# Two transformer blocks on one core: norm steps divided between two engines with order ties, attention and state-space projections in another order, the first loads on another queue, and the last rows in two groups

## The chip, the cores and the metric

One core of a Trainium2 chip. The metric is the time of one execution in microseconds of device time; the kernel before has a median of 2513.2 us over 3 runs (2512.42 to 2513.47).

The core's engines run side by side, each through its own list of instructions in order: TensorE (PE in the rows; its weight loads PEld), VectorE (DVE), ScalarE (ACT), GpSimd (POOL) and SyncE (SP). An engine goes on past an instruction only when what it waits for from the others has come. Loads are issued from a queue, SP's (SPq) or ScalarE's (ACTq).

## What is computed

Two blocks one after the other on one sequence of 256 tokens of width 2048. The parts that the change touches:

```python
# first block
h = rmsnorm(x, g_mix);  z = h @ w_in          # cb, cc, cv, q, k, v, f, gate_c, gate_a
...
x = x + (relu(rmsnorm(x, g_mlp) @ w_ff1) ** 2) @ w_ff2
x = rmsnorm(x, g_final)
# second block
h = rms_norm(x, norm_mix_g) * (1 + scale_m) + shift_m        # h3 in the kernel
q, k, v, xs, z, bmat, cmat, dt = split(h @ w_in_2)
attn = rms_norm(moba_attention(q, k, v, rel_bias), attn_norm_g)
ssm = ssd_mixer(xs, z, bmat, cmat, dt, ...)                  # gated by silu(z), then a norm
x = x + gate_m * (concat([attn, ssm]) @ w_out)
h = rms_norm(x, norm_ffn_g) * (1 + scale_f) + shift_f        # h4 in the kernel
x = x + gate_f * ((silu(g) * val) @ w_down)                  # g, val = conv(h @ w_up)
return rms_norm(x, final_norm_g)
```

`c`'s modulation (shift, scale, gate) comes from `w_ada`. Everything is float32.

## The kernel before

**Products.** Each weight is streamed once, in pieces of 128 x 2048 floats. `piece` (L102) loads one on SP's queue; ScalarE rounds it into `wH` (L122) and VectorE forms the rest `wL` (L123); three buffers of each. An activation is kept as a pair too: `h` and `l`, side by side. `mm` (L129) issues every matmul: a `wH` block against the pair at once (512 columns) and a `wL` block against `h` alone (256 columns, or 512 where the pair lies the other way). `bblock`, `wide` (L186) and `ablock` go over the pieces of a product. In `wide` with `lo_first` all matmuls that need only `h` and `wL` of the first half of the pieces run first.

**The order.** A scheduler lays out each engine's list beforehand, by its own estimate of durations and by a priority of issue. `behind` (L131) adds a tie: an instruction has to come later in the list of its engine than another. `piece` takes such a tie as `hold` for its first quarter's `wL`.

**Start.** `wide` of `cc0` at L443 asks `h1_tiles` (L432) for two 128-row tiles of `x` ahead of each quarter of the first weight piece: a load on SP's queue, then ScalarE's `h` (L436) and VectorE's `l` (L437), both scaled by `g_mix`, the first 16 columns of `vec`. The squares of `x` for the norm (L448 to L456) run at high priority.

**Norms.** `norm2` (L329) makes h3 and h4 from four 512-column chunks of x. Per chunk i: two copies `xc` (L336, VectorE; one for each half t of the tokens) scaled by 1/rms, transposes on TensorE into `trh` (L344), then for each 128-row tile `h` on ScalarE (L350), `nt` on VectorE (L352) and `l = nt - h` on VectorE (L354). 1/rms takes a power on GpSimd (L277, L709). `held` keeps the `l` of tile 7 as a tie for the piece of the second group of k tiles. `conv4` (L714, tiles `bcsp`) is the first user of h3, `up(0)` (L923) of h4.

**Second attention and state space.** Loop L859 goes over j = 0, 1: q and k (each a `bblock`), during each of which `ssm_decay` (tiles `d`, `m`) runs and after it `ssm_out` (tiles `yp`); then v (`ablock`), then `heads` (L421; logits `s`, softmax, transposed `pt`, output `o`, copied to `cat` at L872). `rms_ch` (L829) squares `cat` on ScalarE, adds up on VectorE (L836), sums over channels on TensorE (`rattp`), takes the power on GpSimd, and spreads the result over the partitions (`rattbp`, L282; read back on ScalarE, L284). Then come z0 and z1 (`bblock`, silu at L881, product with `cat` at L883), `cat_split` (L840; scaling at L848, `h` L304, `l` L305; result `catA`), and `wo`, the product with `w_out`, that reads `catA`. `gm_bc` and `gf2` spread modulation over the partitions: 32 transposes (L293) in 8 banks, read by ScalarE (L294).

**End.** `down_last` (L955) does the last four products for both token halves t: `tm` (L970), x (L971), square (L325), product with the final gain (L974), 1/rms, scaling (L980 to L986), and a store of 512 columns each (L987).

Of the kernel before, what the change touches and what calls it, by code (L numbers as in the profile page):

```python
# [25 lines left out]
for _n, _w in (("g_mix", 16), ("b_gate", 32), ("conv_w", 24), ("g_mlp", 16), ("b_ada", 96),  # L26
# [9 lines left out]
def body(ctx: ExitStack, tc: tile.TileContext, x_d, xT_d, vec_d, con_d, rel_d, relc_d, gfin_d, c_d, fg_d,  # L36
# [149 lines left out]
    def wide(W, halves, acts, name, dst, post=None, feed=None, lo_first=False,  # L186
# [13 lines left out]
        for kg in range(2):  # L200
# [128 lines left out]
    def norm2(src, r, av, bv, name):  # L329
        acts = []  # L330
        for i in range(4):
            h, l, hl = act_chunk(name, i)
            xs = []
            for t in range(2):
                xc = tp.tile([P, 512], F32, tag="t2k", bufs=4, name="xc")
                V.tensor_scalar(xc, src[i][:, t, :], r[:, t:t + 1], None,  # L336
                                op0=OP.mult)
                xs.append(xc)
            for b in range(2):
# [6 lines left out]
                for k in range(2):  # L346
# [82 lines left out]
    h1 = []  # L429
    sq0 = []  # L430

    def h1_tiles(h, l, hl, k0, k1):  # L432
        load(xT[:, k0:k1, :], xT_d[:, k0:k1, :])
        for kt in range(k0, k1):
            k = kt % 4
            A.activation(h[:, k, :], xT[:, kt, :], AF.Copy, scale=vc("g_mix", kt))  # L436
            V.scalar_tensor_tensor(l[:, k, :], xT[:, kt, :], vc("g_mix", kt),  # L437
# [8 lines left out]
    load(vec[:, 16:], vec_d[:, 16:])  # L446
    load(con, con_d)
    with tc.high_priority():  # L448
        sacc = junk().rearrange("p (a s) -> p a s", a=2)
        for i in range(8):  # L450
            if i == 0:
                A.activation(sacc, xT[:, 0:2, :], AF.Square)
            else:
                sq = tp.tile([P, 2, S], F32, tag="t2k", bufs=4, name="sq0")
                A.activation(sq, xT[:, 2 * i:2 * i + 2, :], AF.Square)
# [258 lines left out]
    def conv4(nb, ch0, name, first=False):  # L714
        raw = q4([P, 4, S], name + "r")
        if first:
            wide(win2_d, (2 * nb, 2 * nb + 1), h3, name + "p", lambda i: (raw, i), lo_first=True,
                 hold=held["h3"])
# [139 lines left out]

    for j in range(2):  # L859
        qk = []  # L860
# [6 lines left out]
        qT, kT = qk  # L867
# [4 lines left out]
        heads(j, qT, kT, vt, toep, lambda h, o: V.tensor_copy(cat[:, h, :], o))  # L872
# [48 lines left out]
    ss4 = cp.tile([P, 2, 4], F32, name="ss4")  # L921

    def up(j):  # L923
        raw = q4([P, 4, S], f"up{j}r")
        if j == 0:
            wide(wup_d, (0, 1), h4, "up0", lambda i: (raw, i), lo_first=True, hold=held["h4"])
# [28 lines left out]
    def down_last(c, u):  # L955
        ws = [piece(wdn_d[n, c], 4, extra=None if n < 3 else True) for n in range(4)]
        rs4 = cp.tile([P, 2], F32, name="rs4")
        for t in range(2):
            ts = slice(t * P, (t + 1) * P)
            for n in range(4):  # L960
                h, l = ws[n]
                cs = slice(n * 512, (n + 1) * 512)
# [142 lines left out]
```

## Time and profile before

| | us |
|---|---|
| median of 3 runs | 2513.2 |
| the profiled execution | 2515.24 |
| its span (first to last instruction) | 2513.5 |
| TensorE busy | 2481.0 (99%) |
| VectorE busy | 1824.1 (73%) |
| ScalarE busy | 1188.8 (47%) |
| GpSimd busy | 8.0 (0%) |

The columns of a timeline row: start, length, engine, line, operation, out<-in, shapes and how many instructions the row takes together; in brackets the idle time of the engine ahead of it and what ended that. The length of a matmul reaches past the start of the next one: what counts is the distance from start to start. All times are from the span's start.

### The profile page before, as it was taken

Reading aid. Unit: us, or ns where it says so; the run is one execution under the profiler, and the core shown is the slowest. Engines: PE = TensorE matmul, PEld = TensorE weight load, DVE = VectorE, ACT = ScalarE, POOL = GpSimd, SP = SyncE. Lnnn points to the kernel's source line nnn. Section 1 sums busy time; section 2 is a strip of 40 time slices with the busy share of each in tenths; the row PEclk is TensorE's granted clock in tenths of the full one; section 3 lists DMA queues with packets and bytes.
Section 4 is the critical chain, followed back from the end, with each engine's and each line's share of the span. In section 5 each row is a group of like instructions: output and inputs, shape, how many; then the busy total and the mean of one; then the engine's idle time right before and its main releaser. Section 6 shows DMA issues by size and latency. Waiting matters only on the chain.

```text
span 2513.5 us, 31941 instructions
## 1 busy us (share of the span) xinstructions
PE 2481.0 (99%) x13202; PEld 2137.0 (85%) x13202; DVE 1824.1 (73%) x2011; ACT 1188.8 (47%) x1265; POOL 8.0 (0%) x16
## 2 busy tenths in 40 slices
PE   8999999999999999999998999999999999999998
PEld 7888888888888888888887888888888888888887
DVE  6787777787777777777756776575777777777768
ACT  6444444544544444444445544464544444444444
POOL 0000000000000000000000000000000000000000
PEclk9999999999999999999999999999999999999999
DMA  7677776678777777777656444455455555555553
GB/s 283 251 272 282 269 265 254 239 281 315 277 282 278 282 286 271 283 285 280 255 191 210 168 168 161 158 187 198 151 196 192 199 199 187 185 187 195 187 201 118
DMA packets 84977, 573.55 MB, mean 228 GB/s; under 512 B 9368, under 2 KB 10464, under 8 KB 16864
## 3 DMA queue, kind: packets, MB, share of 16 engines
q1 hardware_dynamic: 80352, 564.16, 61.4%
q10 hardware_dynamic: 4480, 7.36, 0.9%
q8 instruction: 103, 1.69, 0.3%
q14 instruction: 42, 0.34, 0.0%
HBM read 567.27 MB, written 4.21 MB: 227 GB/s over the span
## 4 chain that ended last, share of the span: by engine, by line
PE 96%; DVE 2%; ACT 1%; DMA 1%; issue 0%; POOL 0%; SPq 0%; ACTq 0%; POOLq 0%
PE ff L129 27%; PE up L129 20%; PE dn L129 9%; PE ga L129 4%; PE gc L129 4%; PE q L129 4%; PE k L129 4%; PE v L129 3%; PE wo L129 3%; PE mix L129 3%; PE cc L129 3%; PE z L129 2%; PE cb L129 2%; PE co L129 1%; PE ao L129 1%; PE xsc0p L129 1%
## 5 line engine op out<-in xcount | busy, mean ns | idle before, releaser
L123 DVE TENSOR_TENSOR wL<-wraw,wH 128x2048 fp32r<-128x2048 f32 (+1 forms) x511 | 998.5, 1963 | 532.8 <-ACT wH L122 524.1
L122 ACT ACTIVATE wH<-wraw 128x2048 fp32r<-128x2048 f32 (+1 forms) x511 | 837.8, 1653 | 1075.0 <-PE ff L129 359.6
L129 PE MATMUL up<-h4A,wH 128*128 128x512 f32 x1408 | 344.0, 391 | 0.0
L129 PEld LDWEIGHTS up<-h4A,wH 128*128 128x128 f32 x1408 | 256.6, 188 | 48.6 <-DVE up0r L179 0.2
L129 PE MATMUL ff<-g_mlpA,wH 128*128 128x512 f32 x1024 | 250.4, 392 | 0.0
L99 DVE SCALAR_TENSOR_TENSOR wada<-wada,c_bc 128x2048 f32<-128x2048 f32 x96 | 219.6, 2287 | 27.6 <-DMA wada<-in_wada 26.7
L129 PEld LDWEIGHTS ff<-g_mlpA,wH 128*128 128x128 f32 x1024 | 186.6, 188 | 35.7 <-issue 0.6
L129 PEld LDWEIGHTS up<-h4A,wL 128*128 128x128 f32 x1408 | 187.4, 192 | 10.3 <-ACT h4A L350 0.2
L129 PE MATMUL ff<-wH,uh 128*128 128x512 f32 x496 | 193.1, 390 | 0.0
L129 PE MATMUL ff<-wH,ul 128*128 128x512 f32 x496 | 192.9, 389 | 0.0
L129 PE MATMUL up<-h4A,wL 128*128 128x256 f32 x1408 | 191.3, 284 | 0.0
L129 PE MATMUL dn<-wH,vhl 128*128 128x512 f32 x640 | 158.3, 389 | 0.0
L129 PEld LDWEIGHTS ff<-g_mlpA,wL 128*128 128x128 f32 x1024 | 135.4, 191 | 7.4
L129 PEld LDWEIGHTS dn<-wH,vhl 128*128 128x128 f32 x640 | 119.5, 188 | 24.4
L129 PE MATMUL ff<-g_mlpA,wL 128*128 128x256 f32 x1024 | 137.9, 283 | 0.0
L129 PE MATMUL ff<-wL,uh 128*128 128x512 f32 x496 | 127.7, 389 | 0.0
L129 PEld LDWEIGHTS ff<-wH,uh 128*128 128x128 f32 x496 | 93.2, 188 | 19.4 <-issue 0.2
L129 PEld LDWEIGHTS ff<-wH,ul 128*128 128x128 f32 x496 | 93.1, 188 | 19.4 <-issue 0.2
L129 PEld LDWEIGHTS ff<-wL,uh 128*128 128x128 f32 x496 | 93.1, 188 | 19.4
L129 PE MATMUL dn<-wL,vhl 128*128 128x512 f32 x320 | 85.5, 389 | 0.0
L129 PEld LDWEIGHTS dn<-wL,vhl 128*128 128x128 f32 x320 | 60.1, 188 | 12.5
L129 PE MATMUL ga<-h1A,wH 128*128 128x512 f32 x256 | 64.6, 396 | 1.3 <-DVE aos L179 1.3
(559 smaller groups left out, 3172.2 us busy)
## 6 DMA issues: line engine op xcount, KB each, us to landing
wraw<-in_wff SPq DMA_DIRECT2D x128, 1024.0 KB, 4.8
wraw<-in_win SPq DMA_DIRECT2D x106, 1024.0 KB, 4.8
wada<-in_wada SPq DMA_DIRECT2D x96, 1024.0 KB, 4.8
wraw<-in_wup SPq DMA_DIRECT2D x88, 1024.0 KB, 4.8
wraw<-in_wdn SPq DMA_DIRECT2D x44, 1024.0 KB, 4.8
wraw<-in_wv SPq DMA_DIRECT2D x16, 1024.0 KB, 4.8
wraw<-in_wmix SPq DMA_DIRECT2D x16, 1024.0 KB, 4.9
wraw<-in_wout SPq DMA_DIRECT2D x16, 1024.0 KB, 4.8
```

Of the source, the lines that this page charges most:

```text
L99: V.scalar_tensor_tensor(w, w, 1.0, c_bc, op0=OP.mult, op1=OP.mult, accum_out=mod[:, i:i + 1])
L122: A.activation(h[:, sl], raw[:, sl], AF.Copy)
L123: ins = V.tensor_tensor(l[:, sl], raw[:, sl], h[:, sl].bitcast(F32), op=OP.subtract)
L129: return T.matmul(o, l, r, start=first, stop=last, skip_group_check=True)
```

## The change

- **Start.** `g_mix` moves from `vec` into 16 columns in front of `x` (`xTg`), so the small first load is gone. The loads of `x` for k0 = 0 and 2 are issued by ScalarE. The squares of `x` are tied behind the last `h` of `x`.
- **Norms.** In `norm2`, `xc` of the first token half is made by ScalarE for chunks 1 to 3, and `nt` of odd tiles as well. `hold` becomes a pair: the first `wL` of the second half's first piece comes behind `xc` of chunk 0, second token half; the first `wL` of the second group stays behind `l` of tile 7.
- **Second attention.** q0, k0, q1, k1 with their state-space parts come first, then v0, heads 0, v1, heads 1.
- **End.** The last 512 columns of the second token half are computed as two groups of 256; squares are summed in five columns (`ss4`, zeroed at its making), the final gain is multiplied in ahead of the scaling everywhere, and two stores of 1024 columns replace four of 512 for each token half.

```diff
     def wide(...):
             if kg == 0 and lo_first:
-                ws = [piece(W[hf, kg], 4, nt=8) for hf in halves]
+                ws = [piece(W[hf, kg], 4, nt=8, hold=hold[0] if hold and i else None)
+                      for i, hf in enumerate(halves)]
...
-                             hold=hold if kg == 1 and i == 0 else None)
+                             hold=hold[1] if hold and kg == 1 and i == 0 else None)
...
     def norm2(...):
-                V.tensor_scalar(xc, src[i][:, t, :], r[:, t:t + 1], None,
-                                op0=OP.mult)
+                if t == 0 and i > 0:
+                    A.activation(xc, src[i][:, t, :], AF.Copy, scale=r[:, t:t + 1])
+                else:
+                    held[name] = V.tensor_scalar(xc, src[i][:, t, :], r[:, t:t + 1], None,
+                                                 op0=OP.mult)
+                    if i == 0:
+                        held[name + "0"] = held[name]
...
-                    V.tensor_scalar(tt, ps[:, k * S:(k + 1) * S], av[:, kt:kt + 1],
-                                    bv[:, kt:kt + 1], op0=OP.mult, op1=OP.add)
+                    if k:
+                        A.activation(tt, ps[:, k * S:(k + 1) * S], AF.Identity,
+                                     bias=bv[:, kt:kt + 1], scale=av[:, kt:kt + 1])
+                    else:
+                        V.tensor_scalar(tt, ps[:, k * S:(k + 1) * S], av[:, kt:kt + 1],
+                                        bv[:, kt:kt + 1], op0=OP.mult, op1=OP.add)
...
     def h1_tiles(h, l, hl, k0, k1):
-        load(xT[:, k0:k1, :], xT_d[:, k0:k1, :])
+        c0, c1 = (16 if k0 else 0) + k0 * S, 16 + k1 * S
+        if k0 < 4:
+            A.dma_start(xTg[:, c0:c1], xT_d[:, c0:c1])
+        else:
+            load(xTg[:, c0:c1], xT_d[:, c0:c1])
...
-                A.activation(sacc, xT[:, 0:2, :], AF.Square)
+                behind(A.activation(sacc, xT[:, 0:2, :], AF.Square), h1_last[0])
...
+    qk = []
     for j in range(2):
-        qk = []
         for hq, (nb, nm, sc) in enumerate(((0 + j, f"q2{j}", SCALE), (2 + j, f"k2{j}", None))):
...
-        qT, kT = qk
+    for j in range(2):
         ps = ablock(wv2_d, j, range(4), h3, f"v2{j}")
...
-        heads(j, qT, kT, vt, toep, lambda h, o: V.tensor_copy(cat[:, h, :], o))
+        heads(j, qk[2 * j], qk[2 * j + 1], vt, toep, lambda h, o: V.tensor_copy(cat[:, h, :], o))
...
     def down_last(c, u):
+                cuts = ((0, 512),) if t == 0 or n < 3 else ((0, 256), (256, 512))
+                for j, (a, b) in enumerate(cuts):
...
+                    V.tensor_tensor(tm[:, a:b], ps[:, a:b], gf2[:, cs], op=OP.mult)
+                    V.tensor_tensor(x3[:, t, cs], x3[:, t, cs], tm[:, a:b], op=OP.add)
+                    A.activation(junk()[:, a:b], x3[:, t, cs], AF.Square, accum_out=ss4[:, t, n + j:n + j + 1])
+                    if t and n == 3:
+                        y3 = tp.tile([P, 512], F32, tag="t2k", bufs=4, name="y3") if j == 0 else y3
+                        V.tensor_tensor(y3[:, a:b], x3[:, t, cs], fg[:, cs], op=OP.mult)
+                    else:
+                        V.tensor_tensor(x3[:, t, cs], x3[:, t, cs], fg[:, cs], op=OP.mult)
...
-                nc.sync.dma_start(out[0, ts, cs], x3[:, t, cs])
+                if n % 2:
+                    cs = slice((n - 1) * 512, (n + 1) * 512)
+                    nc.sync.dma_start(out[0, ts, cs], x3[:, t, cs])
```

What the scheduler makes of it is seen in the engines' lists, which hold instructions in the order in which they run. First ScalarE from its first instruction, before (`wH_96` and `h1A_85` are the first weight piece and the first four tiles of `x`):

```order
L71 DMA vec<-in_vec 128x16
L88 ACT_TABLE_LOAD
L88 ACTIVATE warm<-mhalf 128x2
L452 ACTIVATE junk<-xT 128x512
L436 ACTIVATE h1A_85<-xT,vec 128x256 x2
L122 ACTIVATE wH_96<-wraw_95 128x512
```

and now (L453 is `h`, L448 the load of `x`):

```order
L448 DMA xT<-in_xT 128x528
L88 ACT_TABLE_LOAD
L88 ACTIVATE warm<-mhalf 128x2
L448 DMA xT<-in_xT 128x512
L122 ACTIVATE wH_95<-wraw_94 128x512
L453 ACTIVATE h1A_84<-xT 128x256 x2
```

The square has left the start, the second load of `x` stands behind the table load, and the first `wH` quarter is now ahead of the first `h`.

VectorE at the step from the first block's end to h3, before (L705 to L708 are sums for the two norms, L651 a square, `wL_10535` the piece of `conv4`'s second half):

```order
L123 TENSOR_TENSOR wL_10535<-wraw_10533,wH_10534 128x512 x2
L705 TENSOR_REDUCE ra<-ssa 128x1
L651 SCALAR_TENSOR_TENSOR sqx,ssb<-xg_10292 128x512
L336 TENSOR_SCALAR xc<-x_4636,rb 128x512
L706 TENSOR_SCALAR re<-ra 128x1
L707 TENSOR_REDUCE rb<-ssb 128x1
L275 TENSOR_SCALAR ra<-ra 128x2
L708 SCALAR_TENSOR_TENSOR rb<-rb,re 128x1
L336 TENSOR_SCALAR xc<-x_4636,rb 128x512 x5
L352 TENSOR_SCALAR nt<-trh_10321,am,mod 128x256
```

and now (L340 is `xc`, L362 `nt`, L722 to L725 the sums):

```order
L668 SCALAR_TENSOR_TENSOR sqx,ssb<-xg_10291 128x512
L340 TENSOR_SCALAR xc<-x_4635,rb 128x512
L722 TENSOR_REDUCE ra<-ssa 128x1
L724 TENSOR_REDUCE rb<-ssb 128x1
L723 TENSOR_SCALAR re<-ra 128x1
L725 SCALAR_TENSOR_TENSOR rb<-rb,re 128x1
L276 TENSOR_SCALAR ra<-ra 128x2
L340 TENSOR_SCALAR xc<-x_4635,rb 128x512 x2
L123 TENSOR_TENSOR wL_10458<-wraw_10456,wH_10457 128x512
L123 TENSOR_TENSOR wL_10534<-wraw_10532,wH_10533 128x512 x3
L340 TENSOR_SCALAR xc<-x_4635,rb 128x512
L362 TENSOR_SCALAR nt<-trh_10320,am,mod 128x256
```

Three quarters of `wL` that stood ahead of the sums, with one more, now stand between the `xc` of the second token half and the first `nt`.

TensorE from the last `o` of `heads` (`pT` against `vt`) to the sum of squares `rattp` of the attention's norm, before:

```order
L129 MATMUL z_0_12717<-h3A_10378,wH_12757 128x512 x4
L129 MATMUL o_12442<-pT,vt_12347 128x256
L129 MATMUL o_12442<-pT,vt_12347 128x128
L129 MATMUL z_0_12717<-h3A_10409,wH_12757 128x512 x4
L129 MATMUL z_0_12717<-h3A_10378,wL_12758 128x256 x4
L129 MATMUL z_0_12717<-h3A_10409,wL_12758 128x256 x4
L129 MATMUL z_1_12798<-h3A_10316,wH_12800 128x512 x8
L129 MATMUL z_1_12798<-h3A_10347,wH_12800 128x512 x8
L129 MATMUL z_1_12798<-h3A_10316,wL_12801 128x256
L129 MATMUL rattp<-con,ratta 128x1 x2
```

and now (`z_1` is the last half block of z, and the last row the first four of the 32 transposes for `gm_bc` and `gf2`):

```order
L129 MATMUL z_1_12797<-h3A_10408,wL_12838 128x256 x4
L129 MATMUL z_1_12797<-h3A_10377,wH_12837 128x512 x4
L129 MATMUL o_12441<-pT,vt_12346 128x256
L129 MATMUL o_12441<-pT,vt_12346 128x128
L129 MATMUL z_1_12797<-h3A_10408,wH_12837 128x512 x4
L129 MATMUL z_1_12797<-h3A_10377,wL_12838 128x256 x4
L129 MATMUL z_1_12797<-h3A_10408,wL_12838 128x256 x4
L129 MATMUL rattp<-con,ratta 128x1 x2
L283 MATMUL rattbp<-con,rattr 128x128 x2
L294 MATMUL gm_bcp_12480<-con,mod 128x128 x4
```

Before, 29 matmuls of z stood between the last `o` and `rattp`, then 36 more up to `rattbp`, and 11 more ahead of the first `wo`, with 28 of the 32 transposes around them. Now 12 stand ahead of `rattp`, none of z comes after it, and `rattbp` follows at once. Between `rattbp` and the first `wo` there are now the 32 transposes and `rss0p` (two matmuls); between the first and the second matmul of `wo` there is `rss0bp`, the spread of the first state-space norm.

## Rows read from the trace of the kernel before

**Rows 1.** The page's chain that ended last: shares of the span by engine.

```profile
PE 96%; DVE 2%; ACT 1%; DMA 1%; issue 0%; POOL 0%; SPq 0%; ACTq 0%; POOLq 0%
```

**Rows 2.** TensorE's waits: line, waited for, total us, times, longest us.

```profile
PE trh L344 <- DVE xc L336: 5.4, 3, 3.1
PE trh L344 <- DVE re L706: 4.3, 1, 4.3
PE yp L129 <- DVE m L806: 2.0, 1, 2.0
```

**Rows 3.** Stretches: length, busy PE, PEld, DVE, ACT, POOL, granted clock, DMA, GB/s.

```profile
1377.00:1384.00 7.00, 4.46 (x20) 4.06 (x21) 5.71 (x19) 2.23 (x5) 1.21 (x2) 0.51 0.22 84
1384.00:1390.00 6.00, 5.93 (x46) 5.35 (x45) 6.00 (x16) 3.66 (x8) 0.00 (x0) 1.00 0.01 3
1766.00:1773.00 7.00, 5.05 (x24) 5.06 (x25) 6.28 (x17) 3.06 (x6) 0.55 (x1) 0.51 0.00 0
```

**Rows 4.** Timeline of the start: TensorE and ScalarE.

```profile
6.20 2.08 PE L129 MATMUL cc<-h1A,wH 128*128 128x512 f32 x4 [6.20 <-ACT wH L122]
...
8.59 4.44 PE L129 MATMUL cc<-h1A,wH 128*128 128x512 f32 x12 [0.31 <-DVE h1A L437]
...
10.96 0.63 ACT L122 ACTIVATE wH<-wraw 128x512 fp32r<-128x512 f32 x1
```

**Rows 5.** Timeline of the step to h3: VectorE, GpSimd, TensorE.

```profile
1376.17 1.28 DVE L123 TENSOR_TENSOR wL<-wraw,wH 128x512 fp32r<-128x512 f32 x2
...
1380.12 2.18 DVE L336 TENSOR_SCALAR xc<-x,rb 128x512 f32<-128x512 f32 x5 [1.27 <-POOL rb L709]
1382.22 0.54 DVE L352 TENSOR_SCALAR nt<-trh,am,mod 128x256 f32<-128x256 f32 x1
...
1383.13 1.99 PE L129 MATMUL bcsp<-h3A,wL 128*128 128x256 f32 x12
...
1378.87 0.70 POOL L277 TENSOR_TENSOR ra<-ra,mhalf 128x2 f32<-128x2 f32 x1 [3.91 <-DVE rb L708]
```

**Rows 6.** Timeline of the step to h4: VectorE.

```profile
1764.60 1.89 DVE L123 TENSOR_TENSOR wL<-wraw,wH 128x512 fp32r<-128x512 f32 x3
...
1767.41 2.18 DVE L336 TENSOR_SCALAR xc<-x,rs 128x512 f32<-128x512 f32 x5 [0.66 <-POOL rs L277]
...
1769.50 0.54 DVE L352 TENSOR_SCALAR nt<-trh,af,mod 128x256 f32<-128x256 f32 x1
```

**Rows 7.** Timeline from the last `o` to `wo`: TensorE, ScalarE, VectorE.

```profile
1656.33 0.81 PE L129 MATMUL o<-pT,vt 128*128 128x256 f32 x4
...
1658.85 3.82 PE L129 MATMUL z<-h3A,wH 128*128 128x512 f32 x16
1662.50 0.28 PE L129 MATMUL z<-h3A,wL 128*128 128x256 f32 x1
1662.62 0.50 PE L129 MATMUL rattp<-con,ratta 128*128 128x1 f32 x4
...
1669.03 1.47 PE L293 MATMUL gm_bcp<-con,mod 128*128 128x128 f32 x12
...
1659.54 1.90 ACT L122 ACTIVATE wH<-wraw 128x2048 fp32r<-128x2048 f32 x1
...
1669.67 1.58 ACT L294 ACTIVATE gm_bc<-gm_bcp 128x512 f32<-128x512 f32 x3
...
1653.86 1.23 DVE L883 TENSOR_TENSOR cat<-cat,zs 128x1024 f32<-128x1024 f32 x1 [1.44 <-ACT zs L881]
...
1661.48 2.29 DVE L123 TENSOR_TENSOR wL<-wraw,wH 128x2048 fp32r<-128x2048 f32 x1 [0.94 <-ACT wH L122]
...
1669.65 3.26 DVE L848 SCALAR_TENSOR_TENSOR cat<-cat,vec,rattb 128x256 f32<-128x256 f32 x8 [2.24 <-ACT rattb L284]
1672.82 0.68 DVE L305 TENSOR_TENSOR catA<-cat,catA 128x512 fp32r<-128x512 f32 x1
```

**Rows 8.** Timeline of the last columns: VectorE.

```profile
2505.74 0.68 DVE L974 TENSOR_TENSOR x<-x,fg 128x512 f32<-128x512 f32 x1
```

More of the change, by code (lines that the diff above doesn't have):

```diff
@@ L25 @@
 _o = 0
-for _n, _w in (("g_mix", 16), ("b_gate", 32), ("conv_w", 24), ("g_mlp", 16), ("b_ada", 96),
+for _n, _w in (("b_gate", 32), ("conv_w", 24), ("g_mlp", 16), ("b_ada", 96),
                ("norm_mix_g", 16), ("attn_norm_g", 8), ("conv_ssm_w", 48), ("conv_ssm_b", 12),
@@ L445, in body @@
          feed=lambda q: h1_tiles(*chunks[q // 2], 2 * q, 2 * q + 2))
-    load(vec[:, 16:], vec_d[:, 16:])
+    load(vec, vec_d)
     load(con, con_d)
@@ L717, in conv4 @@
             wide(win2_d, (2 * nb, 2 * nb + 1), h3, name + "p", lambda i: (raw, i), lo_first=True,
-                 hold=held["h3"])
+                 hold=(held["h30"], held["h37"]))
         else:
@@ L957, in down_last @@
         rs4 = cp.tile([P, 2], F32, name="rs4")
+        ss4 = cp.tile([P, 2, 5], F32, name="ss4")
+        V.memset(ss4, 0.0)
         for t in range(2):
@@ L961, in down_last @@
                 h, l = ws[n]
-                cs = slice(n * 512, (n + 1) * 512)
                 ps = bank(f"dnl{t}{n}")
-                for k in range(4):
-                    mm(ps, u[k][0][:, ts], h[:, k, :], k == 0, False)
-                    mm(ps, u[k][1][:, ts], h[:, k, :], False, False)
-                for k in range(4):
-                    mm(ps, u[k][0][:, ts], l[:, k, :], False, k == 3)
-                tm = tp.tile([P, 512], F32, tag="t2k", bufs=4, name="tm")
-                V.tensor_tensor(tm, ps, gf2[:, cs], op=OP.mult)
-                V.tensor_tensor(x3[:, t, cs], x3[:, t, cs], tm, op=OP.add)
-                ss_chunk(x3[:, t, cs], ss4, t, n)
-                if n < 3:
-                    V.tensor_tensor(x3[:, t, cs], x3[:, t, cs], fg[:, cs], op=OP.mult)
+                cuts = ((0, 512),) if t == 0 or n < 3 else ((0, 256), (256, 512))
+                for j, (a, b) in enumerate(cuts):
+                    for k in range(4):
+                        mm(ps[:, a:b], u[k][0][:, ts], h[:, k, a:b], k == 0 and j == 0, False)
+                        mm(ps[:, a:b], u[k][1][:, ts], h[:, k, a:b], False, False)
+                    for k in range(4):
+                        mm(ps[:, a:b], u[k][0][:, ts], l[:, k, a:b], False, k == 3)
+                    cs = slice(n * 512 + a, n * 512 + b)
+                    tm = tp.tile([P, 512], F32, tag="t2k", bufs=4, name="tm")
+                    V.tensor_tensor(tm[:, a:b], ps[:, a:b], gf2[:, cs], op=OP.mult)
[6 more added lines that the diff above has]
+                        V.tensor_tensor(x3[:, t, cs], x3[:, t, cs], fg[:, cs], op=OP.mult)
             r = rs4[:, t:t + 1]
@@ L979, in down_last @@
                 cs = slice(n * 512, (n + 1) * 512)
-                if n == 3:
-                    V.scalar_tensor_tensor(x3[:, t, cs], x3[:, t, cs], r, fg[:, cs],
-                                           op0=OP.mult, op1=OP.mult)
-                elif n == 1:
-                    V.tensor_scalar(x3[:, t, cs], x3[:, t, cs], r, None, op0=OP.mult)
-                else:
-                    A.activation(x3[:, t, cs], x3[:, t, cs], AF.Copy, scale=r)
-                nc.sync.dma_start(out[0, ts, cs], x3[:, t, cs])
+                src = y3 if t and n == 3 else x3[:, t, cs]
+                if n in (1, 3):
+                    V.tensor_scalar(x3[:, t, cs], src, r, None, op0=OP.mult)
+                else:
+                    A.activation(x3[:, t, cs], src, AF.Copy, scale=r)
+                if n % 2:
+                    cs = slice((n - 1) * 512, (n + 1) * 512)
+                    nc.sync.dma_start(out[0, ts, cs], x3[:, t, cs])
     us = {0: up(0), 1: up(1), 2: up(2)}
```

23 lines of the change are left out of this document (13 added, 10 removed).

## The prediction

> **What bounds the kernel now.** I read the page's chain first: 96% of the span's end hangs on TensorE [rows 1]. So an edit is worth what it takes from TensorE's waits or adds to them, and nothing else that it does to VectorE or ScalarE counts. Next come TensorE's waits by their releaser [rows 2]. Three of them lie where the change works: at the norm steps TensorE waits 5.4 us for `xc` (three times) and 4.3 us for `re`, one of the sums ahead of `xc`; in the second attention it waits 2.0 us for the state-space product `m` (once). Together that is 11.7 us of 2513.5: even a change that took all of it away would be worth 0.5%. Third, the stretches around the two norm steps: the granted clock there is 0.51, the lower of TensorE's two levels (1.2 instead of 2.4 GHz), after TensorE had stood idle [rows 3]. A wait therefore costs more than its length: the first matmuls behind it run slowly. Last I read the timelines around each edit [rows 4 to 8], and beside them the lists of the engines, to see what stands between what is ready and what waits for it.
>
> Times are those of one profiled execution of 2515.24 us, with a span of 2513.5 us. It is 2.0 us above the median of 2513.2 us. I sum against 2515.24 and carry the difference to the median. About 0.2% (5 us: 2508.2 to 2518.2) is what a measurement of this kernel can tell from no change.
>
> **Start: -0.4 us.** Before, the first matmul ran at 6.20 us and the twelve others of the first piece from 8.59 us, behind the second weight quarter; the last quarter's `wH` began at 10.96 us, right after that quarter had landed [rows 4]. Now the two first weight quarters are issued ahead of x on SP, so the second quarter should be there over a microsecond earlier. The other side: ScalarE's first `wH` (0.63 us, as the last one [rows 4]) and VectorE's first `wL` stand ahead of the first `h` and `l`, so the first matmul comes some 0.7 us later, at about 6.9 us. The second x load waits behind ScalarE's table load, but its tiles are needed only from the third quarter on. The end of the piece hangs on the last quarter, and the bytes ahead of it are the same but for the small vector load. I take -0.4, between +0.7 (the first matmul's delay goes through) and -1.0 (part of TensorE's wait between its first four matmuls and 8.59). The squares that leave ScalarE's start took their place while weights were awaited, so they count nothing. The Trainium skill, page "DMA: Bandwidth & Descriptors", section "Issuing engines are not separate DMA queues", says that transfers started by several engines run on the same 16 DMA engines and interleave, and that this saves only the time of issuing. By it the term would be about 0 and the sum 0.4 us higher.
>
> **Step to h3: -0.9 us.** Three quarters of `wL` leave the way to the sums: two take 1.28 us, so three take 1.9 [rows 5]. On GpSimd, the power of `ra` (0.70 us) ran ahead of the one that the norm needs [rows 5]; in the new list it is behind. Part of the two overlaps; `xc` of the second half, at 1380.12 before, comes some 2.3 us earlier, at 1377.8. But now four quarters of `wL` (4 x 0.64 = 2.6 us) stand behind two `xc` (0.43 each, five took 2.18) and ahead of the next `xc` and the first `nt`: 1377.8 + 0.9 + 2.6 + 0.2 = 1381.5, where 1382.22 stood [rows 5]. The tie moved the work from ahead of the norm into its middle. That is 0.7; with half of the `nt` on ScalarE a further 0.2 on the way to the last `l`. Between ends: -2.3 if `wL` there delays nobody, +0.8 if ScalarE, which now makes `xc`, `h` and half of the `nt`, becomes the one that is waited for.
>
> **Step to h4: 0.** Three `wL` (1.89 us) stood ahead of the sums; `xc` followed at 1767.41 and `nt` at 1769.50 [rows 6]. `xc` comes about 0.9 us earlier, since the square on ScalarE bounds it next; then four `wL` (2.6 us) come again ahead of `nt`, which lands at about 1770. ScalarE's share of the later `nt` gives that back. Between -0.9 (all of the gain in `xc`) and +0.8 (all of the delay of `nt`).
>
> **State space in the second attention: -2.0 us.** TensorE waited 2.0 us for `m` [rows 2], where a list of short products had no weight matmuls between `d` and `yp`. Now 64 weight matmuls stand there (half at 0.228, half at 0.12: some 11 us) and no heads run beside. The wait goes whole; nothing bounds TensorE next there.
>
> **Last heads to `wo`: +6.0 us, a new wait.** The heads of j = 1 used to run beside z0, and all of z1 covered what follows them: sum of squares, power, spread, eight scalings, splits. Now heads 0 run beside v1 and z0, heads 1 beside z0 and z1, and only 12 matmuls of z are left behind the last `o`. I put the new list on the clock of before, with the last `o` at 1656.33 [rows 7].
>
> - TensorE: its 12 matmuls end at 1658.85, where z1 began before. What is left to do ahead of the second matmul of `wo` is `rattp` 0.4, `rattbp` 0.2, 32 transposes at 0.10 (twelve in about 1.25) 3.3, `rss0p` 0.4, a `wo` and `rss0bp` 0.4: 4.7 us. If nothing waited, that matmul would run at 1663.5.
> - ScalarE: `rattp`'s sum passes VectorE and GpSimd (0.70, as in [rows 5]) and `rattbp` is done at about 1660.5, but a `wH` stands ahead of the readback, 1659.54 to 1661.44, and a copy from z. The readback ends at 1662.4.
> - VectorE: a `wL` of 2.29 us from 1661.48 stands ahead as well, then 0.69 for z: free at 1664.4. Then the eight scalings 3.26, `cat` times z 1.23, the first split 0.68 [rows 7]: 1669.5.
> - ScalarE beside it: eight readbacks of the transposes and a silu at 0.53 each (three took 1.58) and `h`: 1668. VectorE is last.
>
> 1669.5 - 1663.5 = 6.0. It can't go: with nothing ahead on any engine, power, readback, scalings, product and split take 0.7 + 0.5 + 3.3 + 1.2 + 0.7 = 6.4 us from 1659.3, which is 1665.7 and 2.2 too late. So 2.2 is the lower end; 6.5, if ScalarE's row slips by one operation, is the upper. I take 6.0, since `wH` and `wL` stand in the list ahead.
>
> **The clock behind it: +1.0 us.** The clock fell at both norm steps, where TensorE had stood still or done a few transposes [rows 3]; here it stands or does short transposes for some 10 us. The price of the slow stretch: at the start, twelve matmuls took 0.37 us each from start to start (4.44 with 0.39 for the last) where z runs at 0.228 (16 in 3.65 [rows 7]): 1.7 us in all. At h3 the products ran from 1383.13 [rows 5] and the stretch from 1384 on is at full clock [rows 3], so the loss was under 0.9 x 0.5 = 0.4. I take the middle, 1.0, between 0 and 1.7. The Trainium skill, "TensorE: Matmul & The Clock Gate", section "Loop structure matters more than you think", says that a copy out of PSUM between tiles doesn't let the matmuls go cold. By that the 32 transposes with their readbacks would keep the clock up, and the sum would be 1.0 lower; no row here shows transposes alone doing it.
>
> **End: -0.1 us.** 24 matmuls of 256 columns at 0.12 (1662.50 to 1662.62 [rows 7]) for 12 of 512 at 0.228: +0.15. Behind the last one, `tm` and x are half as long: 0.68 each for 512 columns becomes some 0.35, twice, -0.65 [rows 8]. But a product with the final gain for the first group (about 0.4) comes in between. -0.6 to +0.5.
>
> **The sum.** -0.4 - 0.9 + 0 - 2.0 + 6.0 + 1.0 - 0.1 = +3.6 us: 2518.8 on the profiled execution, **2516.8 us** on the median. That is +0.14%: on the slow side, though mostly not to be told from no change.
>
> **Rivals.** (1) The seam costs its lower end and the clock stays: the sum is -3.4 + 2.2 to 3.7, -1.2 to +0.3, so 2512 to 2513.5. For it: schedules leave slack that I can't see in a list. Against: the `wL` is in the list ahead of the scalings. (2) The change does all that it says: start -1.0, h3 -2.3, h4 -0.9, state space -2.0, end -0.6 are -6.8, and a seam of 2.2 or less leaves -4.6 or more: 2508 or a little under. It needs VectorE's `wL` quarters in the norms to delay nobody. Against it stands that they are listed ahead of the first `nt`. (3) Slower: the clock. If it falls early in the seam and returns only after as long as at h3, where all of 7 us were at 0.51 [rows 3], the dense `wo` matmuls run at half rate for 6 us and more: 3 us or more instead of 1.0, with the seam at 6.5. The sum is -3.4 + 6.5 + 3.0 = +6.1, 2519.3. It decides where the slow stretch covers over 5 us of `wo`. (4) By the skill's rule on queues the start gives nothing: 2517.2, inside my forecast.
>
> **How the numbers follow.** My forecast, 2514 to 2519, gets 0.52, of which 0.10 lies above 2518.2; rival 1 0.22; rival 2 0.10, two thirds of it faster; rival 3 0.16. Faster 0.07 + 0.02 for what I don't see = 0.09; slower 0.10 + 0.16 + 0.02 = 0.28; the same 0.63. The range leaves out most of rival 2 and the upper part of rival 3: 2509.0 to 2520.5.
>
> **What would show it.** In the waits of TensorE: no wait of `yp` for `m`; waits of `trh` down by 2 to 4 us together; new ones of 5 to 7 us in the first matmuls of `wo` for VectorE's `catA`, and `rattbp` waiting for GpSimd for 1 us. In the stretches, a granted clock under 1.00 at about 1665 to 1675. I am wrong if `wo` follows z with under 2 us of waits, or if the clock stays at 1.00 there, or if TensorE waits in a place that I have put at nothing, such as the heads beside z1.

## The result: 0.8% slower, and the profile after

The changed kernel took 2534.76 us (median of 6 runs, 2533.0 to 2537.15) beside 2513.91 us for the kernel before (6 runs). The ratio is 1.0081, with a 95% interval of 1.0068 to 1.0094: 20 us slower, where 3.6 were forecast and 2520.5 was the upper end of the range. The profiled execution took 2533.89 us, with a span of 2532.1 us. One execution of all that were timed for this document, 3082.42 us in the run k3 below, lies far outside the others and is left out of that run's ratio.

I read TensorE's waits first, as before (line, waited for, total us, times, longest us):

```profile
PE cc L129 <- DVE h1A L454: 7.0, 2, 6.6
PE trh L350 <- DVE xc L340: 4.5, 3, 2.3
PE rss0bp L283 <- POOL rss0r L278: 4.1, 1, 4.1
PE trh L350 <- DVE ra L722: 2.6, 1, 2.6
PE wo L129 <- ACT catA L305: 1.9, 1, 1.9
...
PE rattbp L283 <- POOL rattr L278: 1.2, 1, 1.2
```

Against [rows 2], the wait of `yp` for `m` is gone and those of `trh` fell by 2.6 us in all. New are three between the heads and `wo`: 4.1, 1.9 and 1.2, 7.2 us. With these alone (7.2 less 2.0 and 2.6) the time would be 3 us up, not 20. So the rest can't be a wait, and the page's costliest groups show what it is. The kernel before (matmul, shapes, count | busy us, mean ns of one | idle before):

```profile
L129 PE MATMUL up<-h4A,wH 128*128 128x512 f32 x1408 | 344.0, 391 | 0.0
L129 PE MATMUL ff<-wH,ul 128*128 128x512 f32 x496 | 192.9, 389 | 0.0
L129 PE MATMUL up<-h4A,wL 128*128 128x256 f32 x1408 | 191.3, 284 | 0.0
L129 PE MATMUL dn<-wH,vhl 128*128 128x512 f32 x640 | 158.3, 389 | 0.0
```

and the changed kernel:

```profile
L129 PE MATMUL up<-h4A,wH 128*128 128x512 f32 x1408 | 344.5, 392 | 0.1
L129 PE MATMUL up<-h4A,wL 128*128 128x256 f32 x1408 | 187.8, 280 | 0.7 <-ACT h4A L356 0.7
L129 PE MATMUL ff<-wH,ul 128*128 128x512 f32 x496 | 196.3, 396 | 0.0
L129 PE MATMUL dn<-wH,vhl 128*128 128x512 f32 x640 | 162.3, 395 | 0.0
```

The diff touches none of these products, yet a matmul of `dn` lasts 6 ns longer and one of `up` with `wL` 4 ns less. Lengths overlap, so the distance from start to start is the better measure; I took its median from the records of each group. It went from 0.227 to 0.233 us for the 512-column matmuls that stream weights (`ff` with `uh` and `ul`, `dn`, `v`, `mix`, `wo`: some 3,700), from 0.227 to 0.229 for those that stream activations (in the mean under 1 ns), and from 0.120 to 0.118 for those of 256 columns. 6 ns times 3,700 is 22 us; those of 256 columns give some 9 back.

The table has the time between fixed points of the trace (starts of TensorE's matmuls). Two experiments are beside: the changed kernel with its tiles at the addresses of before (p1), and the kernel before with the new attention order alone (k2).

| from the point above to | before | changed | p1 | k2 |
|---|---|---|---|---|
| first `cc` matmul with `wL` | 12.87 | 13.72 | 13.53 | 11.79 |
| last `ff_l` | 1361.06 | 1366.93 | 1359.10 | 1358.47 |
| first `bcsp` with `wH` (step to h3) | 15.30 | 14.06 | 15.57 | 15.49 |
| first `wo` with `wL` (second attention) | 289.07 | 295.31 | 295.30 | 296.97 |
| last `wo` | 84.18 | 86.30 | 83.93 | 83.95 |
| first `up` with `wH` (step to h4) | 14.49 | 13.56 | 15.61 | 14.59 |
| last `dnl` (up and down) | 726.86 | 732.16 | 727.81 | 726.86 |
| end | 9.61 | 10.03 | 10.03 | 9.59 |

Two kinds of loss stand in it. In one place, the second attention, 6 us were lost however the tiles lie. In the long dense stages (to the last `ff_l`, `wo`, up and down), 5.9, 2.1 and 5.3 us were lost, and of that p1 shows only 1.0, in the last stage. The second row also varies by some 2.5 us through a wait for a transfer (`tps`) that the change doesn't touch: 2.1 us in the profile of before, none in k2.

### The profile page after: what moved, and what is told of

The parts are those of the page before. It is cut to its first block, busy times and chain, and to the rows that moved or that the text cites. A ratio compares the mean times of both kernels' runs of the same rounds, so it can differ in the third digit from the quotient of the medians.

```text
span 2532.1 us, 31972 instructions
## 1 busy us (share of the span) xinstructions
PE 2495.5 (99%) x13214; PEld 2128.0 (84%) x13214; DVE 1818.6 (72%) x1995; ACT 1200.0 (47%) x1290; POOL 11.4 (0%) x16
## 4 chain that ended last, share of the span: by engine, by line
PE 96%; DVE 2%; ACT 1%; issue 0%; DMA 0%; POOL 0%; ACTq 0%; POOLq 0%; SPq 0%; DVEq 0%
PE ff L129 27%; PE up L129 19%; PE dn L129 9%; PE wo L129 4%; PE v L129 4%; PE mix L129 4%; PE ga L129 4%; PE k L129 4%; PE gc L129 4%; PE q L129 4%; PE cc L129 3%; PE cb L129 2%; PE z L129 2%; PE co L129 1%; PE ao L129 1%; PE xsc0p L129 1%
## 5 line engine op out<-in xcount | busy, mean ns | idle before, releaser
L655 DVE TENSOR_TENSOR x<-ff,x 128x512 f32<-128x512 f32 x56 | 38.3, 689 | 41.2 <-PE ff L129 41.1
```

Of the source, the lines that this page charges most:

```text
L655: V.tensor_tensor(x1[:, t, cs], ps[t], x1[:, t, cs], op=OP.add)
```

## Experiments

Each was timed beside the kernel before on the same chip, whose medians there were 2516.2 to 2517.0 us; so ratios are used.

### First question: why do untouched matmuls run slower?

The change shortens the small tile `vec` by 64 bytes, enlarges `ss4` (32 bytes more in place) and widens x by 64. Everything behind them in the on-chip memory slides. The addresses in the compiled programs, modulo 256 bytes, of the weight pieces (`wraw`, `wH`, `wL`) and of the activations (all that is kept for TensorE), and the distance from the first to the second:

| kernel | weights | activations | distance |
|---|---|---|---|
| before | 224 | 224 | 0 |
| changed | 192 | 0 | 64 |

**p1, the changed kernel at the places of before.**

```diff
-    xTg = sb.tile([P, 16 + KT * S], F32, tag="xs", name="xT")
+    xTg = sb.tile([P, 128 + KT * S], F32, tag="xs", name="xT")
...
-    mhalf = cp.tile([P, 2], F32, name="mhalf")
+    mhalf = cp.tile([P, 10], F32, name="mhalf")[:, 0:2]
```

> The changed kernel, the same instructions in the same order, with two tiles made wider so that the weight pieces and all the activations lie at the places of the kernel before (address modulo 512 bytes: 224 for both; in the changed kernel 192 and 256). Theory P (the change moved tiles by 32 bytes in the on-chip memory, and the pace of matmuls depends on the place): the matmuls of ff and dn with the weights as the moving operand go back from 0.233 to 0.227 us, those of 256 columns from 0.118 to 0.120, and the time falls by some 14 us, to 2521. Theory O (the new order or the new load queue sets the pace): 0.233 stays, 2534 to 2535 us.

2521.79 us, ratio 1.0022 (1.0012 to 1.0031). The page's rows of `ff` with `ul` (192.9 us, 389 ns) and `dn` (158.3 us, 389 ns) are those of before again. Some 0.6%, 15 us, were the places; 5.5 us (3 to 8) are what the change itself costs.

**p2, the kernel before at the places of the changed one.** Its two 8-byte tiles share one allocation and x is 64 bytes wider.

> The kernel before, the same instructions in the same order, with its tiles at exactly the addresses of the changed kernel (two 8-byte tiles merged, x made 64 bytes wider). Theory P: ff and dn go from 0.227 to 0.233 us, 256 columns from 0.120 to 0.118, and the time rises by some 14 us, to 2528. Theory O: 2513 to 2515 us, 0.227 stays.

2530.87 us, ratio 1.0053 (1.0038 to 1.0068), with `dn` at 395 ns and 0.233 us from start to start. The slow pace comes without any of the change's steps.

**p3 and p4, one of the two moved.** p3 widens x by 32 bytes; p4 takes 32 bytes out ahead of the weights and puts them back behind.

> The kernel before with only the activations moved by 32 bytes (modulo 512: weights 224, activations 256). Theory P with the moving operand deciding: ff and dn, which move weights, stay at 0.227, and the 256-column matmuls, which move activations, go to 0.118: some 9 us faster, 2505. Theory P with the distance between the two operands deciding: ff and dn go to about 0.233 as well, about 2528. Theory O: 2514.

> The kernel before with only the weight pieces moved by 32 bytes (modulo 512: weights 192, activations 224). Theory P with the moving operand deciding: ff, dn, v, mix and wo at 0.233, 256 columns at 0.120: about 2537. With the distance between the operands deciding: like the kernel with only the activations moved. Theory O: 2514.

2546.48 us (1.0116, 1.0099 to 1.0133) and 2547.26 us (1.0119, 1.0104 to 1.0134). My first form of the theory fell: the moving operand's own place doesn't decide, since both kernels have the same pace, 0.233 to 0.234 for 512 columns and 0.117 for 256, and both have a distance of 32.

**p5 to p8, the distance.** p5 moves everything by 32 bytes; p6, p7 and p8 move the activations by 128, 64 and 256 bytes.

> The kernel before with everything moved by 32 bytes together (weights and activations both at 256 modulo 512, distance 0). If the distance between the two operands of a matmul decides: 512 columns at 0.227, 256 columns at 0.120, time as before, 2514 to 2517. If the place itself decides (activations at 256 made the 256-column matmuls 0.118 or 0.117, weights off 224 made ff and dn 0.233): at least one of the two changes, 2505 to 2530.

> The kernel before with only the activations moved, by 128 bytes (weights 224, activations 352 modulo 512). If the distance decides modulo 64 or 128: the pace of before, 0.227, about 2515. If it decides modulo 512: another pace; nothing measured so far says which, 2505 to 2547.

> The kernel before with only the activations moved, by 64 bytes (weights 224, activations 288: the distance of the changed kernel, 64, from another base). If the distance decides: as with the changed kernel's own places, ff and dn 0.233, up 0.229, 256 columns 0.118, about 2531. If the base decides: something else.

> The kernel before with only the activations moved, by 256 bytes (weights 224, activations 480 modulo 512). If the pace repeats with 256 bytes: 0.227 and 0.120, about 2515. If it repeats only with 512: slower, 2530 to 2550.

The medians from start to start, in us:

| distance modulo 256 | kernels | 512, weights stream | 512, activations stream | 256 | time against before |
|---|---|---|---|---|---|
| 0 | before, p1, p5, p8 | 0.227 | 0.227 | 0.120 | p5 0.9999 (0.9990 to 1.0008); p8 2515.4 us, one run |
| 64 | changed, p2, p7 | 0.233 | 0.229 | 0.118 | p2 1.0053; p7 2529.7 us, one run |
| 32 | p3, p4 | 0.233 | 0.234 | 0.117 | 1.0116, 1.0119 |
| 128 | p6 | 0.231 | 0.232 | 0.119 | 1.0122 (1.0105 to 1.0139) |

Ten kernels, and the distance alone sorts them: a common shift (p5) and one by 256 (p8) change nothing, the same distance from another base (p7) gives the changed kernel's pace.

**p9, which tiles' distance.** A gap of 32 bytes between the two groups of activations.

```diff
+    sb.tile([P, 8], F32, tag="gap", bufs=1, name="gap")
     chunks = [act_chunk("h1", i) for i in range(4)]
```

> The kernel before with a gap of 32 bytes between the two groups of activation tiles: uh, ul and vhl (the stationary operand of ff_2 and dn) stay at the distance 0 from the weights, h1, h3, h4, g_mlp, mg and cat move to distance 32, and so do the small temporary tiles. If the distance between the two operands of the matmul decides: dn and ff with uh and ul stay at 0.227, while up, ff with g_mlp, gc and ga go to 0.234 and 0.117, and mix, wo and v to 0.233: some 22 us more than before (18 from the 512-column products of up, ff, gc, ga, q, k, cb, cc, less 13 from those of 256 columns, plus 7 from v, mix and wo: 10 to 22). If the temporary tiles that ScalarE and VectorE write decide: dn and ff with uh go to 0.233 too.

2531.02 us, ratio 1.0055 (1.0038 to 1.0071). The page:

```profile
L129 PE MATMUL up<-h4A,wH 128*128 128x512 f32 x1408 | 349.7, 395 | 0.1
L129 PE MATMUL dn<-wH,vhl 128*128 128x512 f32 x640 | 158.3, 389 | 0.0
L129 PE MATMUL ff<-wL,uh 128*128 128x512 f32 x496 | 127.7, 389 | 0.0
```

`dn` and `ff` kept their 389 ns and 0.227, though the temporary tiles that ScalarE and VectorE write were moved; `up` went to 395 and 0.234, `mix` and `wo` to 0.233 and 0.235. It is the two operands of the matmuls that count.

**p10, whose matmul.** Only `wL` is moved, by 32 bytes modulo 256 (a tile of 96 bytes ahead of it in a pool of three buffers, and x widened by 224 so that the activations stay).

> The kernel before with only wL moved, by 32 bytes modulo 256, against everything else; wH and the activations keep the distance 0. If each matmul's own operands decide: products with wH stay at 0.227, those of 256 columns with wL go to 0.117, and those of 512 columns with wL (ff, dn, v, mix, wo) to 0.233: -13 us for the first, +8 for the second, about 5 us less than before. If neighbouring matmuls act on each other (the weight load of one beside the reads of the other): products with wH change as well, 2515 to 2545 us.

2532.48 us, ratio 1.0064 (1.0049 to 1.0079), and the products with `wH`, whose operands hadn't moved, changed too:

```profile
L131 PE MATMUL ff<-wH,ul 128*128 128x512 f32 x496 | 194.0, 391 | 0.0
L131 PE MATMUL dn<-wH,vhl 128*128 128x512 f32 x640 | 161.0, 393 | 0.0
```

From start to start `dn` with `wH` went to 0.231, `up` with `wH` to 0.230, 256 columns only to 0.118. For `mix`, `v` and `wo` with `wH` the median stayed at 0.227 to 0.228. Read matmul by matmul, those with `wH` that follow one with `wL` are the ones that change: in `mix` the medians of the first seven are 0.241, 0.224, 0.231, 0.236, 0.228, 0.232 and 0.231, and from the eighth on it is 0.227 again. So neighbouring matmuls act on each other. The weight load of one runs while another streams: in the second stretch of [rows 3], PE and PEld are each busy for over 5 of 6 us. That the two meet in the memory is what fits; it was not measured apart, and why 256 columns go faster where 512 go slower stays open.

### Second question: what does the new order cost?

**k1, the old attention order in the changed kernel (at the places of before).**

```diff
     for j in range(2):
+        qk = []
...
-    for j in range(2):
+        qT, kT = qk
         ps = ablock(wv2_d, j, range(4), h3, f"v2{j}")
...
-        heads(j, qk[2 * j], qk[2 * j + 1], vt, toep, lambda h, o: V.tensor_copy(cat[:, h, :], o))
+        heads(j, qT, kT, vt, toep, lambda h, o: V.tensor_copy(cat[:, h, :], o))
```

> The changed kernel at the places of before (2521.8 us with the reordered attention), with the loop of the second attention as it was: q, k, v, heads for each half. If the new wait between the heads and wo is what the order itself costs: no wait of wo and of the state-space norm's spread for GpSimd (about 7.5 us of waits go, and half a microsecond to 1.5 us of slow clock), the wait of 2.2 us in the state space comes back: 2514 to 2516. If the loss lies in the norms, the start or the end: 2520 and more.

2515.56 us, ratio 0.9995 (0.9986 to 1.0005), so -1.3 us (-3.5 to +1.3). The other three parts of the change, the norms, the start and the end, together come to nothing that can be measured.

**k2, the new order alone, in the kernel before.** The same edit the other way round.

> The kernel before with only the loop of the second attention changed (all q and k first), its places as they were. If the order costs what the other run gave back: 6 us more than before, with waits of wo for catA and of the state-space norm's spread for GpSimd, and no wait of yp for m. If the cost needs the new norms or the new start beside it: 2 us less than before.

2521.97 us, ratio 1.0025 (1.0014 to 1.0035), with the same three waits as the changed kernel and none of `yp`. The order alone costs what p1 costs.

**k3, the state-space norm's power ahead of VectorE's run.** In the changed kernel, TensorE's list of the seam read (start, length, what it waited for):

```profile
1671.45 0.50 PE L129 MATMUL rattp<-con,ratta 128*128 128x1 f32 x4
1673.10 0.43 PE L283 MATMUL rattbp<-con,rattr 128*128 128x128 f32 x2 [1.15 <-POOL rattr L278]
1673.37 1.91 PE L294 MATMUL gm_bcp<-con,mod 128*128 128x128 f32 x16
1675.12 2.00 PE L294 MATMUL gf2p<-con,mod 128*128 128x128 f32 x16
1676.95 0.60 PE L129 MATMUL rss0p<-con,rss0a 128*128 128x1 f32 x4
1679.45 0.50 PE L129 MATMUL wo<-wH,catA 128*128 128x512 f32 x1 [1.89 <-ACT catA L305]
1684.01 0.69 PE L283 MATMUL rss0bp<-con,rss0r 128*128 128x128 f32 x2 [4.07 <-POOL rss0r L278]
1684.35 5.83 PE L129 MATMUL wo<-wH,catA 128*128 128x512 f32 x15
```

and beside it VectorE and GpSimd:

```profile
1673.75 2.29 DVE L123 TENSOR_TENSOR wL<-wraw,wH 128x2048 fp32r<-128x2048 f32 x1 [0.72 <-ACT wH L122]
1675.95 0.68 DVE L179 TENSOR_TENSOR zs<-z,lo 128x512 f32<-128x512 f32 x1
1676.56 3.25 DVE L865 SCALAR_TENSOR_TENSOR cat<-cat,vec,rattb 128x256 f32<-128x256 f32 x8
1679.72 0.15 DVE L276 TENSOR_SCALAR rss0r<-rss0p 128x2 f32<-128x2 f32 x1
1679.79 1.21 DVE L900 TENSOR_TENSOR cat<-cat,zs 128x1024 f32<-128x1024 f32 x1
1680.92 2.49 DVE L306 TENSOR_TENSOR catA<-cat,catA 128x512 fp32r<-128x512 f32 x4
...
1679.95 4.01 POOL L278 TENSOR_TENSOR rss0r<-rss0r,mhalf 128x2 f32<-128x2 f32 x1 [6.90 <-DVE rss0r L276]
```

The power of two columns that takes 0.7 to 1.1 us elsewhere took 4.01. It began 0.16 us after VectorE's product of two tiles (L900) and ended 0.55 us after the last split (1680.92 + 2.49). In the kernel before the same power took 0.69 us, where it began 0.15 us ahead of that product.

```diff
+        if name == "rss0":
+            guard.append(V.tensor_copy(cp.tile([P, 2], F32, name="seen"), r))
...
-        V.tensor_tensor(cat[:, sl, :], cat[:, sl, :], z, op=OP.mult)
+        gated = V.tensor_tensor(cat[:, sl, :], cat[:, sl, :], z, op=OP.mult)
+        if j == 1:
+            behind(gated, guard[0])
...
+            if i < 2:
+                behind(low, guard[0])
```

> The changed kernel at the places of before (2521.8 us), with VectorE made to wait for the power of the first state-space norm before it multiplies cat by z and splits (a copy of two columns that reads the power's result). Theory L (GpSimd's power, 4.01 us instead of 0.70, was held off by VectorE's unbroken run of operations on two tiles): the power takes 0.7 us, its spread comes some 3.3 us earlier, the second matmul of wo some 1.6 us earlier, and the time falls by 1 to 2.5 us. Theory S (the power is slow by itself here): 4 us again, and the time rises by about 3 us, since VectorE waits too.

2517.99 us, ratio 1.0011 (1.0002 to 1.0020), where p1 had 1.0022. GpSimd and TensorE now:

```profile
1671.12 0.69 POOL L278 TENSOR_TENSOR rss0r<-rss0r,mhalf 128x2 f32<-128x2 f32 x1 [6.87 <-DVE rss0r L276]
...
1670.62 0.50 PE L129 MATMUL wo<-wH,catA 128*128 128x512 f32 x1 [1.89 <-ACT catA L305]
1671.86 0.43 PE L283 MATMUL rss0bp<-con,rss0r 128*128 128x128 f32 x2 [0.74 <-POOL rss0r L278]
1673.79 6.42 PE L129 MATMUL wo<-wH,catA 128*128 128x512 f32 x15 [1.50 <-DVE catA L306]
```

The power is not slow by itself; it was held off. Not every run of VectorE does that to the end. In the kernel before, the power of the second state-space norm began 0.16 us after the first of two splits and ended at 1689.68, a little ahead of the second one (1689.73), which had begun 0.44 us after it:

```profile
1688.45 1.28 DVE L305 TENSOR_TENSOR catA<-cat,catA 128x512 fp32r<-128x512 f32 x2
1688.61 1.07 POOL L277 TENSOR_TENSOR rss1r<-rss1r,mhalf 128x2 f32<-128x2 f32 x1 [9.49 <-DVE rss1r L275]
```

Why it was let in there between two operations, and in the changed kernel only behind the last of five, stays open. Making VectorE wait 0.8 us for it brought `wo`'s second matmul from 4.9 us behind the first to 3.2. In this execution the slow clock took part of that back: the fifteen matmuls behind took 6.27 us, in p1 5.10, and the stage of the second attention as a whole is only 0.6 us shorter (294.7 to 295.3). The rest of the difference in the profiles lies elsewhere: 1.5 us at the step to h3, where the lists are the same. So the cause of the 4 us is shown, and that removing it gains about 3 us is not.

**k4, a version that beats both.** Only q of the second half goes ahead of the first half's v and heads.

```diff
+    proj(0, 0)
+    proj(0, 1)
+    proj(1, 0)
+    attend(0)
+    proj(1, 1)
+    attend(1)
```

(`proj` is q or k with its state-space part, `attend` v and heads, as in the loop.)

> The kernel before with one step moved: q of the second half ahead of v and heads of the first half (q0, k0, q1, v0, heads 0, k1, v1, heads 1). The list of TensorE then has the old 29 matmuls of z behind the last o and no heads beside q1. If the wait of yp for m goes and no other comes: 2 us less than before. If the heads beside k1 now run late: new waits there or behind the last o, 0 to 3 us more.

2512.65 us, ratio 0.9987 (0.9978 to 0.9996). There is no wait of `yp`, none at `wo`, and the stage of the second attention takes 286.8 us instead of 289.07. What the reorder was to bring is had by moving one projection, since heads 1 still run beside z0 and z1 still covers the norm.

The gain by the ratio, 3.3 us (1.0 to 5.5), may be more than the wait of 2.0 us, and the clock gives a reason. In k1 that wait ended at 1578.11, and behind it the granted clock (the column ahead of the last two) was 0.57 for a while:

```profile
1579.00:1583.00 4.00, 4.00 (x12) 3.08 (x11) 2.58 (x4) 1.19 (x2) 0.00 (x0) 0.57 0.60 238
```

Six of the eleven profiles with the old order show such a stretch within 1.6 us of that wait; the profile of before happens not to. None of the four with the new order shows one, nor does k4.

## Why the prediction was wrong, step by step

**The step that failed** is one that the sum didn't have: it took every matmul that the diff doesn't touch at its old duration. The places of the tiles changed; some 3,700 matmuls of 512 columns came 6 ns further apart and some 4,500 of 256 columns 2 ns closer. p1 and p2 put that at 13 to 15 us of the 20. That the tiles move can be had from the sizes of `vec`, `ss4` and x, if one adds them up; what it costs only the runs show.

**The rest of the sum** was +3.6 us, and p1, where the places are the old ones, measures 5.5 (3 to 8). Its two parts hold as well: the order alone was forecast at -2.0 + 6.0 + 1.0 = +5.0 and k2 measures +6.3 (3.5 to 8.8); start, norms and end were forecast at -1.4 and k1 measures -1.3 (-3.5 to +1.3). For the second part that is in some measure luck, since in p1's profile the rows of start, norms and end add up to +3.4, and the row up to `ff_l`, where nothing was forecast, takes 2.0 back. The terms, by p1's trace:

- Start: -0.4 forecast, +0.7 in the table's row for p1. The second weight quarter came earlier, as said (ScalarE rounded it at 7.22 us, before at 7.92), but VectorE's `wL` stood ahead of `l`, so the twelve matmuls behind the first four waited for `h1A` and began at 9.03 us in the changed kernel where [rows 4] had 8.59:

```profile
6.59 2.07 PE L129 MATMUL cc<-h1A,wH 128*128 128x512 f32 x4 [6.59 <-DVE h1A L454]
7.22 0.63 ACT L122 ACTIVATE wH<-wraw 128x512 fp32r<-128x512 f32 x1 [1.01 <-DMA wraw<-in_win]
...
8.49 1.66 DVE L454 SCALAR_TENSOR_TENSOR h1A<-xT,h1A 128x256 fp32r<-128x256 f32 x4
9.03 4.86 PE L129 MATMUL cc<-h1A,wH 128*128 128x512 f32 x12 [0.36 <-DVE h1A L454]
```

  What I had set as the upper end, that the first matmul's delay goes through, is what came in this execution: 0.39 us at the first matmul, 0.44 at the twelve. The other 0.4 us of the changed kernel's row are pace: its matmuls stood 0.43 us apart until 13.0 us, those of before until 11.7, and 0.23 behind that. The second load of x did not wait for the table load, as I had put it: it was issued at 1.25 us, while the table load ran from 1.18 to 2.46. But the row of the table scatters: 11.8 to 14.0 us in twelve kernels with the old start, 12.5 to 13.7 in four with the new one. So this term can't be told from nothing.
- State space: -2.0, and the wait of `yp` is gone in every kernel with the new order and in k4.
- Seam: +6.0, measured 1.15 + 1.89 + 4.06 = 7.1 us of waits. The mechanism was right up to the first split: the `wL` and the eight scalings ran as put on the clock of before, and the split ended 5.5 us after it was due. But the second matmul of `wo` was not kept waiting by VectorE's `catA`, as forecast. The sum counts `rss0p` and `rss0bp` and gives the power between them no time, so it put a wait of `rss0bp` for GpSimd at nothing; a wait in such a place was one of its own signs of being wrong. Held off by VectorE, that power was the last to come, 2.4 us behind the split.
- Clock: +1.0 with 1.7 as the upper end; the fifteen `wo` matmuls after the seam took 5.10 us from start to start in p1 instead of 3.4, so 1.7. In the changed kernel it was 2.2, and in k2 (6.18) 2.8. The granted clock there (stretch, length, busy PE, PEld, DVE, ACT, POOL, clock, DMA share, GB/s):

```profile
1672.00:1676.00 4.00, 2.90 (x27) 2.82 (x27) 3.17 (x5) 4.00 (x7) 0.82 (x1) 1.00 0.48 202
1676.00:1680.00 4.00, 2.05 (x15) 1.50 (x13) 4.00 (x12) 4.00 (x9) 0.05 (x1) 1.00 0.70 242
1680.00:1684.00 4.00, 0.00 (x0) 0.00 (x0) 3.41 (x5) 1.37 (x3) 3.96 (x1) 0.77 0.07 25
1684.00:1686.00 2.00, 1.99 (x6) 1.70 (x7) 0.84 (x3) 1.26 (x4) 0.00 (x0) 0.50 0.00 0
1686.00:1688.00 2.00, 2.00 (x6) 1.52 (x6) 2.00 (x6) 1.29 (x3) 0.00 (x0) 0.50 0.00 0
1688.00:1690.00 2.00, 2.00 (x8) 1.61 (x7) 1.04 (x3) 0.00 (x0) 0.00 (x0) 0.76 0.00 0
```

  These are the changed kernel's. Through the 32 transposes with their readbacks (1673.37 to 1676.95) the clock stayed at 1.00 (first two rows), and it fell in the 4 us without a matmul behind them (third row). It also fell after less: in k3, where no wait of the seam was over 1.89 us, and in k2 ahead of the same 4 us, so that it was down for the whole of them:

```profile
1672.00:1676.00 4.00, 0.10 (x1) 0.00 (x0) 3.56 (x6) 1.52 (x4) 3.90 (x1) 0.50 0.08 31
```

- The page "TensorE: Matmul & The Clock Gate" of the Trainium skill, that I weighed in the prediction (section "Loop structure matters more than you think", a copy out of PSUM between tiles leaves the matmuls warm), agrees with the first two of the changed kernel's rows; the loss came behind the transposes, which it does not speak of.
- Norms: -0.9 and 0 forecast; in p1 +0.3 and +1.1. `wL` did move into the middle of the norm, as said:

```profile
1384.75 0.88 DVE L340 TENSOR_SCALAR xc<-x,rb 128x512 f32<-128x512 f32 x2 [0.59 <-POOL rb L726]
1385.55 2.49 DVE L123 TENSOR_TENSOR wL<-wraw,wH 128x512 fp32r<-128x512 f32 x4
1387.95 0.48 DVE L340 TENSOR_SCALAR xc<-x,rb 128x512 f32<-128x512 f32 x1
1388.35 0.54 DVE L362 TENSOR_SCALAR nt<-trh,am,mod 128x256 f32<-128x256 f32 x1
```

  This is the changed kernel at the step to h3; against [rows 5], `xc` comes 4.1 us after the last `ff_l` began instead of 6.2, and the first `nt` 7.7 instead of 8.3. What the step takes in all goes with how long the clock stays down: 14.06 us in the changed kernel, 15.57 in p1, with the same lists and a granted clock of 0.77 and 0.74 from 1383 to 1390 in the one, of 0.50 and 0.65 from 1378 to 1386 in the other. At h4 it took 13.56 and 15.61, and 13.59 in k1. The forecast of next to nothing holds; the sizes scatter by more than they are.
- End: -0.1 forecast. The stage from `up` on took 1.0 us more in p1 and k1 than before, and the rest 0.4 more. Half of the first shows as a wait that I hadn't seen: the second group of 256 columns goes to the same tile `dnl` as the first and waits until VectorE has read it (here in the changed kernel; 0.5 us in p1 and k1 too).

```profile
2518.52 1.59 PE L129 MATMUL dnl<-wHL,vhl 128*128 128x256 f32 x12
2520.15 0.42 DVE L990 TENSOR_TENSOR tm<-dnl,gf 128x256 f32<-128x256 f32 x1 [0.54 <-PE dnl L129]
2520.63 1.69 PE L129 MATMUL dnl<-wHL,vhl 128*128 128x256 f32 x12 [0.52 <-DVE tm L990]
```

**The rivals.** The third, slower through a longer slow clock, had the right sign and, for the seam, the right place; its 1.7 to 2.8 us of clock are a tenth of what was lost. None of the four knew of the pace.

## What to carry to other kernels

Add up the sizes of the tiles that a change resizes, and look at the addresses that result, before its steps are priced: in this kernel 32 bytes of distance between the operands cost 29 us (p3) and all the steps of the change together 5.5 (p1). After a run, compare the mean length of the groups that the change doesn't touch first; if these moved, put the tiles back and measure again. When a fill of independent work is moved, look for what it covered: here one projection moved ahead is a gain of 0.13%, two a loss of 0.25%.

## What the runs showed of the hardware

- The pace of back-to-back fp32 matmuls, with 128x128 weights loaded for each, depends on the distance between the addresses of the tile that is loaded and the tile that streams, and repeats after 256 bytes (p8, one run): 512 columns every 0.227 us at distance 0, 0.229 to 0.236 at 32, 64 and 128; 256 columns every 0.120 at 0 and 0.117 to 0.119 elsewhere. Neighbours count as well: with `wL` alone moved, the matmuls with `wH` that follow one with `wL` change too (p10). The Trainium skill, page "SBUF — State Buffer", section "Who interferes with whom", calls TensorE's two read ports, one for the moving operand and one for weight loads, independent, and the shared pair of VectorE and GpSimd the only cause of contention. By that the distance should cost nothing; in p3 and p4 it costs 1.2% of the time, in p9 0.5%, and these decide. Where the two operands meet is not shown.
- A GpSimd operation on two columns took 4.01 us instead of 0.70 where VectorE had just begun an unbroken run of five operations on two tiles, and 0.69 where it began first. The same section of the Trainium skill says that a VectorE operation with two inputs in SBUF and a GpSimd operation that reads SBUF exclude each other; k3 agrees. In the 4.01 us the wait lasted for the whole run of operations; behind two splits (1.07 us) it did not, and by the records that power and the second split ran side by side.
- TensorE's clock stayed at its upper level through 32 short transposes spread over 3.6 us. Behind them it fell: in the changed kernel within the 4 us without a matmul, in k2 ahead of these, and in k3 with no wait of the seam over 1.89 us.
